# Two-layer diffusion trunk with 32 experts: adders and gathers in one work block per pair, a shorter layer step, full-width loads of the output weights

## The chip, the cores and the metric

One core of one Trainium2 chip runs the whole program. The time is in device microseconds (us) of one launch. The kernel before takes 1481.97 us, the median of 3 runs (1481.2 to 1482.17).

## What is computed

A trunk of two layers over 256 latent and 256 context tokens of width 1024, all in float32. Cut to what matters here:

```python
for i in range(2):                        # with_ctx_out = i < 1
    sh1, sc1, g1, sh2, sc2, g2 = split(silu(c) @ w_mod[i] + b_mod[i], 6)
    hl = modulate(rms_norm(x, norm1_g[i]), sh1, sc1)       # the same for xc with c_ctx
    lat_mix, ctx_mix = token_mixers(hl, hc, w_in[i], ..., sink[i], cos, sin, with_ctx_out)
    x = x + g1 * (lat_mix @ w_out[i])                      # 6 + 6 heads of 64 and 256 conv channels
    hl = modulate(rms_norm(x, norm2_g[i]), sh2, sc2)       # in layer 0 also the context
    y = hierarchical_moe(hl, w_group[i], b_group[i], w_expert[i], ..., w_gate[i], w_up[i], w_down[i])
    x = x + g2 * y                                         # top-1 of 4 groups, top-2 of its 8 experts
return rms_norm(x, final_g)
...
def run(xb, e):                            # for each expert
    return (silu(xb @ w_gate[e]) * (xb @ w_up[e])) @ w_down[e]
```

## The kernel before

The program is Python that emits instructions for the five engines; a scheduler puts them in order where no manual schedule is given. In layer 1 only the latent tokens go through the output projection and the experts.

**Storage.** `slot` hands out eight buffers of 1 MB in turn; nearly all weights pass through them, loaded on SP's queue in program order. Smaller loads use a pool of 512 KB tiles (`load_k4`). A weight's load waits for the last reader of its buffer.

**Number formats.** Exact float32 products run as float32 matmuls. Others split both sides into a high part that the faster format (`fp32r`) holds and the rest, and sum three products (high by high, high by low, low by high): `Splits` makes the parts of a weight on ACT (`wh`) and on DVE or POOL (`wl`).

**Startup.** Eleven small tables (the rotary table, then for each layer the q and k gains, two router biases and the sinks) are loaded on POOL's queue (L194 to L207), the sinks' negation `negsink` on POOL at L210. SP loads the first layer's modulation weights (`wm`), and in between `wkv` and `wU`, the weights of the first projections. `mod_load(...)` issues a modulation's loads and returns `compute`, which multiplies (`pm`, L281) and adds the bias. Between the two halves of layer 0's first modulation stand 20 dummy products (L584 to L586). The router's weights `wr` are loaded on POOL at each layer's start (L471, L472), though first read after the attention.

**Attention and output projection.** A unit takes two heads, j and 3 + j, of a group. `load_wo` (L922 to L933) therefore gathers the rows of w_out in nine loads, eight of them 64 partitions wide, at the end of SP's queue for this part.

**Experts.** 16 pairs a layer, in eight quads of two pairs; each pair streams 12 MB. `pair` multiplies gate (`pgu`, 32 machine products), then up, transposes the activations (`pat`), and multiplies down (`py`). Four bursts of other work stand in between: after gate, after up, after the transposes and half way through down. The list `at` (L1587 to L1596) fills them with the adders of the pair before (`row_adders`: per 128 output channels two products `pc` and two updates of the residual `xT` on DVE) and the gathers of the next quad's tokens (`pg`, L1285, L1286; ACT copies them to `xg`).

**Layer step.** The last pair of layer 0 goes through `finish` (L1533 to L1546): after each adder the residual is squared on ACT; POOL adds squares 1 to 3 to 0, and sums over channels are taken of five squares (`ss`, L418; four products each, which the trace counts as eight). Then comes layer 1's norm, `rb` (the norm spread over partitions), modulated tokens `hT`/`hL`, and the first projection `pkv` (L558). The modulation (1, 2), called `early`, fills TensorE's gaps.

Of the kernel before, what the change touches and what calls it, by code (L numbers as in the profile page):

```python
# [15 lines left out]
OP = mybir.AluOpType  # L16
# [20 lines left out]
def trunk(ctx: ExitStack, tc: tile.TileContext, t_in, rope, out, cfg):  # L37
# [156 lines left out]
    gp.dma_start(rope_t, rope)  # L194

    def bcast_load(t, src, n):
        gp.dma_start(t, bass.AP(tensor=src.tensor, offset=src.offset, ap=[[0, 128], [1, n]]))

# [3 lines left out]
    for l in range(DEPTH):  # L202
        bcast_load(gqk[:, l, 0, :], qg_d[l], 64)
        bcast_load(gqk[:, l, 1, :], kg_d[l], 64)
        bcast_load(rb[:, l, 0:4], bgrp_d[l], 4)
        bcast_load(rb[:, l, 4:36], bexp_d[l], 32)
        bcast_load(sinkb[:, l, :], sink_d[l], 6)  # L207
# [55 lines left out]
    def mod_load(l, m, c0, nc, load=load_k):  # L263
# [9 lines left out]
        def compute(two=False, eng=gp, between=None, p=None):  # L273
# [3 lines left out]
            for k in range(KC * nq // 4):  # L277
                for q in range(4):
                    kq = k + q // nq * 4
                    c = q % nq * n  # L280
                    pe.matmul(p[0][32 * q:32 * q + 32], scT[:, kq, :], ws[128 * kq // nr][:, kq % (nr // 128), c:c + n],  # L281
                              start=k == 0, stop=k == KC * nq // 4 - 1)
            s = K2("ms", (128, n), tag="m")
# [23 lines left out]

        return compute
# [99 lines left out]
    sums, ss1 = [], []  # L408
# [50 lines left out]
    def layer(l):  # L459
# [5 lines left out]
        r1 = rstd(ssq0 if l == 0 else ss1[0], 4, D, "n1")  # L465
        if l > 0:
            finish_mods(l, 1)
# [3 lines left out]
        gp.dma_start(wr[:, :, 0:4], wgrp_d[l].rearrange("(k p) g -> p k g", p=128))  # L471
        gp.dma_start(wr[:, :, 4:36], wexp_d[l].rearrange("(k p) g -> p k g", p=128))  # L472
        h_mul, h_scale, h_shift, hH, hL = modulate(l, r1)
# [21 lines left out]
        if l > 0:  # L495
            early = mod_load(*todo.pop(0), 0, 8)
        for j in range(4):
# [38 lines left out]
        if l > 0:  # L536
            h_mul(0)
            h_scale(0)
            ws = Splits(wKV, 512)
            trans.close()  # L540
            with tc.high_priority(offset=-cfg["fpri"]):
                early(True)
# [20 lines left out]
        if l == 0:  # L563
# [16 lines left out]

            modulation(0)
            mul_to(3)

            for _ in range(20):  # L584
# [1078 lines left out]
```

## Time and profile before

| | |
|---|---|
| median of 3 runs | 1481.97 us (1481.2 to 1482.17) |
| profiled execution: time, span | 1484.51 us, 1482.9 us |
| mean granted TensorE clock | 0.979 of full |
| busy: PE, DVE, ACT, POOL | 1410.0, 612.1, 394.6, 85.9 us |
| moved by DMA | 481.86 MB, mean 325 GB/s |

The span runs from the first to the last instruction of the profiled execution; some 1.6 us lie around it. Busy time is a mean over stages with different limits: the startup and layer 0's projections to about 150 us, attention and output projection to 297, layer 0's experts from 305 to 803, the layer step to 823, layer 1's mixers and router to 1020, and layer 1's experts to the end.

### The profile page before, as it was taken

Reading aid. Unit: us, or ns where it says so; the run is one execution under the profiler, and the core shown is the slowest. Engines: PE = TensorE matmul, PEld = TensorE weight load, DVE = VectorE, ACT = ScalarE, POOL = GpSimd, SP = SyncE. Lnnn points to the kernel's source line nnn. Section 1 sums busy time; section 2 is a strip of 40 time slices with the busy share of each in tenths; the row PEclk is TensorE's granted clock in tenths of the full one; section 3 lists DMA queues with packets and bytes.
Section 4 is the critical chain, followed back from the end, with each engine's and each line's share of the span. In section 5 each row is a group of like instructions: output and inputs, shape, how many; then the busy total and the mean of one; then the engine's idle time right before and its main releaser. Section 6 shows DMA issues by size and latency. Waiting matters only on the chain. (4 is left out here: it accounts for less than half of the span.)

```text
span 1482.9 us, 20526 instructions
## 1 busy us (share of the span) xinstructions
PE 1410.0 (95%) x8080; PEld 775.2 (52%) x8080; DVE 612.1 (41%) x1379; ACT 394.6 (27%) x954; POOL 85.9 (6%) x146
## 2 busy tenths in 40 slices
PE   6999899999999999998999998989999999999997
PEld 4777677754444544444435776774443343333432
DVE  3469884353223333333334568853222222222223
ACT  3454575430111111100102555652111111110102
POOL 3212000100000000000001020010000000000000
PEclk8999999999999999999999899999999999999999
DMA  9847502399799999999999583087999999999996
GB/s 312 315 156 260 138 2 103 153 359 371 319 402 411 415 409 407 417 408 397 390 401 383 203 292 89 4 361 290 371 419 422 420 421 422 421 420 421 420 418 257
DMA packets 92324, 481.86 MB, mean 325 GB/s; under 512 B 8884, under 2 KB 17296, under 8 KB 47040
## 3 DMA queue, kind: packets, MB, share of 16 engines
q1 hardware_dynamic: 90960, 478.19, 81.3%
q0 software_dynamic: 800, 1.20, 0.4%
q8 instruction: 66, 1.08, 0.3%
q10 hardware_dynamic: 464, 1.11, 0.2%
q14 instruction: 34, 0.28, 0.0%
HBM read 479.42 MB, written 1.05 MB: 324 GB/s over the span
## 5 line engine op out<-in xcount | busy, mean ns | idle before, releaser
L1340 PE MATMUL pgu<-we,xg 128*64 128x512 f32 x1904 | 450.8, 598 | 23.4 <-DMA we<-in_w_gate_dram 13.1
L1340 PEld LDWEIGHTS pgu<-we,xg 128*64 128x64 f32 x1904 | 143.5, 137 | 308.8 <-issue 251.6
L1394 PE MATMUL py<-we,actT 128*64 128x512 f32 x888 | 205.8, 597 | 0.7 <-ACT actT L1355 0.7
L1236 DVE SCALAR_TENSOR_TENSOR xT<-pc,mod,xT 128x256 f32<-128x256 f32 x256 | 104.8, 476 | 177.4 <-PE pc L1233 177.4
L1394 PEld LDWEIGHTS py<-we,actT 128*64 128x64 f32 x888 | 61.9, 136 | 114.8 <-issue 110.8
L1290 ACT COPY xg<-pg 128x256 f32<-128x256 f32 x112 | 36.3, 376 | 309.8 <-PE pg L1286 309.8
L1349 DVE SCALAR_TENSOR_TENSOR act<-pgu,ws,sil 128x512 f32<-128x512 f32 x32 | 24.0, 751 | 194.0 <-PE pgu L1340 185.1
L1244 DVE TENSOR_TENSOR xo<-xo,pc 128x512 f32<-128x512 f32 x62 | 39.8, 683 | 111.3 <-PE pc L1243 111.3
L1285 PE MATMUL pg<-OH,hH 128*128 128x256 f32 x336 | 84.2, 290 | 0.0
L1286 PE MATMUL pg<-OH,hL 128*128 128x256 f32 x336 | 81.7, 283 | 0.0
L634 DVE SCALAR_TENSOR_TENSOR ca<-gpad,cw,ca 128x512 f32<-128x512 f32 (+1 forms) x120 | 73.3, 611 | 0.9
L1285 PEld LDWEIGHTS pg<-OH,hH 128*128 128x128 f32 x336 | 64.2, 191 | 11.4 <-issue 10.5
L281 PE MATMUL pm<-wm,scT 128*32 128x256 f32 (+1 forms) x896 | 64.3, 370 | 2.2 <-DMA wm<-in_w_mod_dram 2.0
L1286 PEld LDWEIGHTS pg<-OH,hL 128*128 128x128 f32 x336 | 64.3, 191 | 0.0
L1344 ACT ACTIVATE sil<-pgu 128x512 f32<-128x512 f32 x32 | 19.2, 598 | 167.1 <-PE pgu L1340 167.1
L1259 DVE TENSOR_TENSOR Yg<-py,g2r 128x512 f32<-128x512 f32 x31 | 21.3, 688 | 100.8 <-PE py L1394 96.5
L1363 POOL CAST se<-ident 32x128 fp32r<-32x128 f32 x32 | 9.1, 286 | 900.8 <-PE pb L1364 871.0
L1261 ACT CAST YH<-py 128x512 fp32r<-128x512 f32 x32 | 18.7, 586 | 151.3 <-PE py L1394 134.4
L1261 ACT CAST YH<-Yg 128x512 fp32r<-128x512 f32 x31 | 19.1, 618 | 141.2 <-DVE Yg L1259 141.2
L1232 PE MATMUL pc<-oht,YH 128*128 128x512 f32 x128 | 55.2, 432 | 0.2 <-ACT YH L1261 0.2
L1233 PE MATMUL pc<-oht,YL 128*128 128x512 f32 x128 | 50.6, 395 | 0.2 <-DVE YL L1262 0.2
L1262 DVE TENSOR_TENSOR YL<-py,YH 128x512 fp32r<-128x512 f32 x32 | 22.1, 691 | 61.2 <-ACT YH L1261 61.2
(434 smaller groups left out, 2125.4 us busy)
## 6 DMA issues: line engine op xcount, KB each, us to landing
we<-in_w_up_dram SPq DMA_DIRECT2D x112, 1024.0 KB, 8.9
we<-in_w_down_dram SPq DMA_DIRECT2D x111, 1024.0 KB, 11.2
we<-in_w_gate_dram SPq DMA_DIRECT2D x110, 1024.0 KB, 11.8
wm<-in_w_mod_dram SPq DMA_DIRECT2D x44, 1024.0 KB, 11.0
wp<-in_w_gate_dram SPq DMA_DIRECT2D x8, 1024.0 KB, 11.2
wp<-in_w_up_dram SPq DMA_DIRECT2D x8, 1024.0 KB, 10.3
we<-in_w_gate_dram SPq DMA_DIRECT2D x16, 512.0 KB, 11.0
we<-in_w_up_dram SPq DMA_DIRECT2D x16, 512.0 KB, 10.2
```

Source lines behind the costliest of these rows:

```text
L281: pe.matmul(p[0][32 * q:32 * q + 32], scT[:, kq, :], ws[128 * kq // nr][:, kq % (nr // 128), c:c + n], start=k == 0, stop=k == KC * nq // ...
L634: ve.scalar_tensor_tensor(a, g, wt, a, op0=OP.mult, op1=OP.add)
L1232: pe.matmul(pc, YH[:, 128 * o:128 * o + 128], oht, start=True, stop=False)
L1233: pe.matmul(pc, YL[:, 128 * o:128 * o + 128], oht, start=False, stop=True)
L1236: ve.scalar_tensor_tensor(xT[:, o, sl], pc[:, sl], mod[l][:, 5, o, s:s + 1], xT[:, o, sl], op0=OP.mult, op1=OP.add)
L1244: ve.tensor_tensor(xo[t][:, sl], xo[t][:, sl], pc, op=OP.add)
L1261: sc.copy(YH[:rows, sl], py)
L1285: pe.matmul(dst, hH[t][:, 128 * k:128 * k + 128], rhs, start=t == 0, stop=False)
L1286: pe.matmul(dst, hL[t][:, 128 * k:128 * k + 128], rhs, start=False, stop=t == NT - 1)
L1290: sc.copy(xg[e][:, k - 1:k + 1, :], v[:, :, e])
L1340: pe.matmul(p[64 * e:64 * e + 64, m, :], xg[:, k, 64 * e:64 * e + 64], w_[e](k % 4), start=k == 0, stop=k == KC - 1)
L1394: pe.matmul(py[64 * e:64 * e + 64, h], actT[:, 128 * f + 64 * e:128 * f + 64 * e + 64], wd[e](f % 2)[:, 512 * h:512 * h + 512], start=f == ...
```

## The change

**Experts of layer 0**, the 13 pairs from the second to the fourteenth that gather for a next quad: gate and up run as one piece, down as one piece. All eight adders stand with the gathers between up and the down product: after up two adders, two gathers and two adders, after the transposes one adder, the other two gathers and three adders. The first pair, the last quad and layer 1 keep their order.

**Startup.** The eleven small loads go to SP, behind the last `wU`; `negsink` comes two operations later on POOL. Of the dummies 4 stand before the second half of the modulation and 12 after it. `wr` is loaded on SP ahead of `wo`.

**Heads** 2j and 2j + 1 make a unit, so w_out's rows are contiguous: five loads of 128 partitions in place of nine.

**Layer step.** The loads of modulation (1, 2) are named earlier (their place in SP's order is the same), its products stand between the sums; square 4 is added on POOL and squares 5 and 6 on DVE, so three squares are summed, not five; the weight splits of the first projection stand ahead of the norm; eight dummy products (`warm`) precede the first projection.

Core of the diff:

```diff
-    gp.dma_start(rope_t, rope)
...
-        gp.dma_start(t, bass.AP(tensor=src.tensor, offset=src.offset, ap=[[0, 128], [1, n]]))
...
-    gp.tensor_scalar(negsink, sinkb.rearrange("p l (h j) -> p l j h", h=2), -1.0, None, op0=OP.mult)
+    def bcast_load(t, src, n, eng=gp):
+        eng.dma_start(t, bass.AP(tensor=src.tensor, offset=src.offset, ap=[[0, 128], [1, n]]))
+
+    def small_inputs():
+        sp.dma_start(rope_t, rope)
+        for l in range(DEPTH):
+            bcast_load(gqk[:, l, 0, :], qg_d[l], 64, sp)
...
+            bcast_load(sinkb[:, l, :], sink_d[l], 6, sp)
+        gp.tensor_scalar(negsink, sinkb.rearrange("p l (j h) -> p l j h", h=2), -1.0, None, op0=OP.mult)
@@ mod_load
-        def compute(two=False, eng=gp, between=None, p=None):
+        def products(ks=range(KC * nq // 4), two=False, p=None):
...
+        def compute(two=False, eng=gp, between=None, p=None, made=None):
+            p = made or products(two=two, p=p)
@@ layer
-        gp.dma_start(wr[:, :, 0:4], wgrp_d[l].rearrange("(k p) g -> p k g", p=128))
-        gp.dma_start(wr[:, :, 4:36], wexp_d[l].rearrange("(k p) g -> p k g", p=128))
...
+        if l == 0:
+            small_inputs()
...
+        if l > 0:
+            ws = Splits(wKV, 512)
+        h_mul, h_scale, h_shift, hH, hL = modulate(l, rstd(ss1[0] if l else ssq0, 4, D, "n1"))
...
         if l > 0:
+            early[0].products(range(5, 8), p=early[1])
+            pw_ = P1("warm")
+            for _ in range(8):
+                pe.matmul(pw_[:, 0:256], identb, masks.rearrange("p a b -> p (a b)"), start=True, stop=True)
...
-                early(True)
+                early[0](made=early[1])
...
             modulation(0)
             mul_to(3)
-
-            for _ in range(20):
-                pe.matmul(pm[:, 1, 256:512], identb, masks.rearrange("p a b -> p (a b)"), start=True, stop=True)
+            dummies(4)
             modulation(1)
+            dummies(12)
@@ unit
-                    q = qT[g](3 * h + j, 128 * (i + b))
+                    q, kv = qT[g](2 * j + h, 128 * (i + b)), (2 * j + h) // 3
@@ load_wo
-            for n, part in enumerate((((0, 0, 2),), ((0, 128, 1), (1, 640, 1)), ((0, 704, 2),))):
-                for h in range(2):
-                    for i, r, m in part:
-                        r += 192 * h
-                        sp.dma_start(t[n][64 * h:64 * h + 64, i:i + m, :], src[r:r + 64 * m].rearrange("(j d) f -> d j f", d=64))
-            sp.dma_start(t[3], src[384:640].rearrange("(c p) f -> p c f", p=128))
+            for n in range(4):
+                c0, c1 = order[2 * n:2 * n + 2]
+                if c1 == c0 + 1:
+                    sp.dma_start(t[n], src[128 * c0:128 * c0 + 256].rearrange("(c p) f -> p c f", p=128))
+                else:
+                    for i, c in enumerate((c0, c1)):
+                        sp.dma_start(t[n][:, i], src[128 * c:128 * c + 128])
...
+        sp.dma_start(wr[:, :, 0:4], wgrp_d[l].rearrange("(k p) g -> p k g", p=128))
+        sp.dma_start(wr[:, :, 4:36], wexp_d[l].rearrange("(k p) g -> p k g", p=128))
         wo = load_wo()
@@ finish
-                    if o in (1, 2, 3):
+                    if o in (1, 2, 3, 4):
                         gp.tensor_tensor(sq_[0], sq_[0], q, op=OP.add)
+                    if o == 6:
+                        ve.tensor_tensor(q, sq_[5], q, op=OP.add)
                 if h == 1:
+
+                    f = mod_load(*todo.pop(0), 0, 8)
+                    made = f.products(range(2), two=True)
                     p = P1("ss1")
-                    for i, o in enumerate((0, 4, 5, 6, 7)):
-                        sum_tokens(p, sq_[o], NT, i == 0, i == 4)
+                    for i, o in enumerate((0, 7, 6)):
+                        sum_tokens(p, sq_[o], NT, i == 0, i == 2)
+                    f.products(range(2, 5), p=made)
@@ the bursts of a pair
-                    at = [adders[:3] + mine[:hot] if qd or e else [weights], mine[hot:6], adders[3:5], adders[5:]]
-                    at[3] += mine[6:]
-                    if not mine:
-                        at[1], at[2] = at[2], []
+                    if mine and not last:
+
+                        g = mine[hot:]
+                        head, g = (g[:1], g[1:]) if hot else ([], g)
+                        a_ = adders
+                        at = [mine[:hot], head + a_[:2] + g[:2] + a_[2:4],
+                              a_[4:5] + g[2:4] + a_[5:6] + g[4:6] + a_[6:7] + g[6:] + a_[7:], []]
+                    else:
...
```

How the order of instructions changes, at three places. The names are those of the tiles: `pgu` gate and up, `pc` adders, `pg` gathers, `pat` transposes, `pb` the pair's slots, `py` down.

PE, a second pair of a quad in layer 0, before:

```order
L1340 MATMUL pgu<-we,xg 64x512 x16
L1232 MATMUL pc<-oht,YH 128x512
L1233 MATMUL pc<-oht,YL 128x512
...
L1340 MATMUL pgu<-we,xg 64x512 x16
L1285 MATMUL pg<-OH,hH 128x256
L1286 MATMUL pg<-OH,hL 128x256
...
L1353 MATMUL pat<-ident,act 128x128 x4
L1232 MATMUL pc<-oht,YH 128x512
...
L1364 MATMUL pb<-posT,se 128x512
L1394 MATMUL py<-we,actT 64x512 x8
L1232 MATMUL pc<-oht,YH 128x512
...
L1394 MATMUL py<-we,actT 64x512 x8
```

and with the change:

```order
L1354 MATMUL pgu<-we,xg 64x512 x32
L1246 MATMUL pc<-oht,YH 128x512
L1247 MATMUL pc<-oht,YL 128x512
...
L1299 MATMUL pg<-OH,hH 128x256
L1300 MATMUL pg<-OH,hL 128x256
...
L1246 MATMUL pc<-oht,YH 128x512
...
L1367 MATMUL pat<-ident,act 128x128 x4
L1246 MATMUL pc<-oht,YH 128x512
...
L1299 MATMUL pg<-OH,hH 128x256
...
L1246 MATMUL pc<-oht,YH 128x512
...
L1378 MATMUL pb<-posT,se 128x512
L1408 MATMUL py<-we,actT 64x512 x16
```

Gate and up are one run of 32 products, and down one of 16 (the trace counts two machine products for each); the adders stand on both sides of the gathers in the one block between them.

PE, the layer step from the last down product to the first projection (`pm` modulation, `ss` sums of squares, `rb` the norm; the trace counts two machine products for each of `pm` and `ss`), before:

```order
L1370 MATMUL py<-we,actT 64x512 x4
L281 MATMUL pm<-wm,scT 32x256 x8
L1232 MATMUL pc<-oht,YH 128x512
...
L418 MATMUL ss_6622<-ones,sq 128x1 x4
L281 MATMUL pm<-wm,scT 32x256 x8
L418 MATMUL ss_6622<-ones,sq 128x1 x12
L281 MATMUL pm<-wm,scT 32x256 x3
L418 MATMUL ss_6622<-ones,sq 128x1 x4
L281 MATMUL pm<-wm,scT 32x256 x13
L339 MATMUL rb<-ident,n1r 128x128 x4
L291 MATMUL pm<-ident,ms 128x8 x2
L558 MATMUL pkv<-wh,hT 128x512 x4
```

and with the change, from the last adder on:

```order
L1246 MATMUL pc<-oht,YH 128x512
L1247 MATMUL pc<-oht,YL 128x512
L281 MATMUL pm<-wm,scT 32x256 x8
L423 MATMUL ss_6633<-ones,sq 128x1 x12
L281 MATMUL pm<-wm,scT 32x256 x12
L344 MATMUL rb<-ident,n1r 128x128 x4
L281 MATMUL pm<-wm,scT 32x256 x12
L542 LDWEIGHTS identb
L542 MATMUL warm<-masks,identb 128x256
...
L563 MATMUL pkv<-wh,hT 128x512 x2
L295 MATMUL pm<-ident,ms 128x8 x2
```

The sums are 12 in one piece, `rb` stands between two runs of 12 modulation products, and the dummies between the second run and `pkv`.

SP's queue ahead of the output projection, as the difference:

```order
 L85 DMA wm<-in_w_mod_dram 128x2x1024 x12
-L930 DMA wo<-in_w_out_dram 64x2x1024 x2
-L930 DMA wo<-in_w_out_dram 64x1024 x4
-L930 DMA wo<-in_w_out_dram 64x2x1024 x2
-L931 DMA wo<-in_w_out_dram 128x2x1024
-L1007 DMA xs<-in_w_down_dram 128x2048
+L978 DMA wr<-in_w_group_dram 128x8x4
+L979 DMA wr<-in_w_expert_dram 128x8x32
+L940 DMA wo<-in_w_out_dram 128x2x1024
+L943 DMA wo<-in_w_out_dram 128x1024 x2
+L940 DMA wo<-in_w_out_dram 128x2x1024 x2
```

The two loads of `wr` now come first, and each load of `wo` spans 128 partitions.

## Rows read from the trace of the kernel before

**Rows 1.** The page, traffic in 40 slices of 37 us, GB/s.
```profile
GB/s 312 315 156 260 138 2 103 153 359 371 319 402 411 415 409 407 417 408 397 390 401 383 203 292 89 4 361 290 371 419 422 420 421 422 421 420 421 420 418 257
```

**Rows 2.** Windows: length, busy us by engine (PE first), then PEclk, DMA share, GB/s.
```profile
498.47:529.47 31.00, 31.00 (x160) 14.80 (x157) 10.86 (x24) 3.56 (x8) 0.28 (x1) 1.00 1.00 406
529.47:559.58 30.11, 30.11 (x152) 13.91 (x150) 9.34 (x20) 3.56 (x8) 0.28 (x1) 1.00 1.01 414
1100.00:1350.00 250.00, 237.55 (x1075) 98.55 (x1073) 56.56 (x99) 30.75 (x69) 2.58 (x9) 1.00 1.01 421
```

**Rows 3.** Timeline of PE, pairs of layer 0: start, us, line, operation, tiles, count.
```profile
331.78 4.08 PE L1394 MATMUL py<-wp,actT 128*64 128x512 f32 x17 [0.25 <-ACT actT L1355]
338.70 0.60 PE L1340 MATMUL pgu<-we,xg 128*64 128x512 f32 x2
...
505.77 0.39 PE L1233 MATMUL pc<-oht,YL 128*128 128x512 f32 x1
506.00 0.39 PE L1232 MATMUL pc<-oht,YH 128*128 128x512 f32 x1
...
514.04 1.05 PE L1311 MATMUL pw<-whl,OH 128*128 128x4 f32 x8
520.81 3.65 PE L1394 MATMUL py<-we,actT 128*64 128x512 f32 x16
```

**Rows 4.** DMA view, 438 to 678 us (layer 0's experts), 40 slices of 6 us, GB/s.
```profile
GB/s 406 429 423 421 359 403 430 418 422 410 385 423 429 418 377 386 422 429 421 411 392 423 426 422 396 389 415 429 418 423 396 429 422 422 406 369 393 427 422 427
```

**Rows 5.** DMA view, 4 to 30 us, the POOL queue: packets, MB, share of 16 engines.
```profile
q0 software_dynamic: 576, 0.52, 17.1%
```

**Rows 6.** Startup: timeline of PE, ACT, SP and POOL, and one window (as rows 2).
```profile
21.95 4.01 PE L585 MATMUL pm<-masks,identb 128*128 128x256 bf16 x20 [0.26 <-DVE mod L298]
...
30.52 0.40 ACT L526 CAST wu<-wU 128x256 fp32r<-128x256 f32 x1 [0.76 <-DMA wU<-in_w_in_dram]
...
31.39 0.50 PE L558 MATMUL pkv<-wh,hT 128*128 128x512 f32 x1 [1.85 <-ACT hT L365]
...
39.73 1.84 SPq L91 DMA_DIRECT2D wU<-in_w_in_dram  x1
...
54.23 0.74 POOL L527 TENSOR_TENSOR wu<-wU,wu 128x256 fp32r<-128x256 f32 x1 [5.70 <-ACT wu L526]
...
32.50:36.00 3.50, 3.50 (x10) 2.71 (x9) 0.00 (x0) 0.00 (x0) 0.00 (x0) 0.51 1.05 387
```

**Rows 7.** Output weights: waits of 150 to 166, timeline of ACT, DMA from 144 to 172.
```profile
PE pT L843 <- ACT P L829: 5.2, 2, 4.1
...
158.66 1.14 ACT L380 CAST wh<-wo 128x512 fp32r<-128x512 f32 x2 [3.77 <-DMA wo<-in_w_out_dram]
...
GB/s 386 351 363 357 363 316 380 351 392 369 211 222 181 199 246 205 252 228 228 211 275 205 211 263 240 205 263 211 205 211 228 269 193 334 287 82 29 0 0 0
```

**Rows 8.** Layer step: timeline of DVE, PE and ACT, and the window of half clock.
```profile
806.03 3.22 DVE L1236 SCALAR_TENSOR_TENSOR xT<-pc,mod,xT 128x256 f32<-128x256 f32 x8 [0.59 <-PE pc L1233]
...
809.10 3.78 PE L418 MATMUL ss<-ones,sq 128*128 128x1 f32 x24
809.35 0.63 ACT L412 ACTIVATE sq<-xT 128x512 f32<-128x512 f32 x1 [0.15 <-DVE xT L1236]
...
813.81 1.87 PE L418 MATMUL ss<-ones,sq 128*128 128x1 f32 x8
...
815.61 3.62 PE L281 MATMUL pm<-wm,scT 128*32 128x256 f32 x26
...
819.16 1.12 PE L339 MATMUL rb<-ident,n1r 128*128 128x128 f32 x4
...
822.98 2.07 PE L558 MATMUL pkv<-wh,hT 128*128 128x512 f32 x4 [2.05 <-ACT wh L380]
...
810.80:827.80 17.00, 14.95 (x70) 10.78 (x70) 7.42 (x20) 6.06 (x15) 0.33 (x1) 0.50 1.04 369
```

**Rows 9.** DMA view of 806 to 816, 40 slices of 0.25 us, GB/s.
```profile
GB/s 451 328 434 340 397 397 328 381 340 365 352 352 344 352 348 344 352 344 348 352 373 254 332 213 139 250 139 213 305 285 285 334 365 346 422 352 350 358 371 371
```

More of the change, by code (lines that the diff above doesn't have):

```diff
@@ L276, in compute @@
                 p = p[:, 0:n], p[:, n:n + 16]
-            for k in range(KC * nq // 4):
+            for k in ks:
                 for q in range(4):
@@ L306, in compute @@
                 eng.tensor_tensor(A, A, g[:, :, None].to_broadcast([128, nc, 2]), op=OP.mult)
+        compute.products = products
         return compute
@@ L406, in trunk @@
     count = {}
-    sums, ss1 = [], []
+    sums, ss1, early = [], [], []
     def square(k, nt):
@@ L579, in splits, with dummies @@
                 su[k] = split_u(k, 0)
+            def dummies(n):
+                for _ in range(n):
+                    pe.matmul(pm[:, 1, 256:512], identb, masks.rearrange("p a b -> p (a b)"), start=True, stop=True)
             modulation(0)
             mul_to(3)
-            for _ in range(20):
-                pe.matmul(pm[:, 1, 256:512], identb, masks.rearrange("p a b -> p (a b)"), start=True, stop=True)
+            dummies(4)
             modulation(1)
+            dummies(12)
             splits(0)
@@ L805, in unit @@
                 for h in range(2):
-                    q = qT[g](3 * h + j, 128 * (i + b))
+                    q, kv = qT[g](2 * j + h, 128 * (i + b)), (2 * j + h) // 3
                     masked = g == 1 and i < 2
                     o, ks = (S[:, h, :], slice(0, 512)) if i < 2 else (S[:, h, 256 * b:256 * b + 256], slice(256, 512))
-                    pe.matmul(o, q, kH[g][:, h, ks], start=True, stop=False)
-                    pe.matmul(o, q, kL[g][:, h, ks], start=False, stop=not masked)
+                    pe.matmul(o, q, kH[g][:, kv, ks], start=True, stop=False)
+                    pe.matmul(o, q, kL[g][:, kv, ks], start=False, stop=not masked)
                     if masked:
@@ L860, in unit @@
             ve.tensor_tensor(rs, po[:, 0:nq], rs, op=OP.mult)
-            mh = qT[g](j, 128 * i, nq)
+            mh = qT[g](2 * j, 128 * i, nq)
             sc.copy(mh, rs)
-            ve.tensor_tensor(qT[g](3 + j, 128 * i, nq), rs, mh.bitcast(F32), op=OP.subtract)
+            ve.tensor_tensor(qT[g](2 * j + 1, 128 * i, nq), rs, mh.bitcast(F32), op=OP.subtract)
         conv(len(taps))
@@ L883, in mixed @@
             g, j = c // 5, c % 5
-            return qT[g](j, 0, N), qT[g](3 + j, 0, N)
+            return qT[g](2 * j, 0, N), qT[g](2 * j + 1, 0, N)
         def chunked(a):
@@ L1589, in layer @@
                     hot = 1 if len(mine) > 4 else 0
-                    at = [adders[:3] + mine[:hot] if qd or e else [weights], mine[hot:6], adders[3:5], adders[5:]]
-                    at[3] += mine[6:]
-                    if not mine:
-                        at[1], at[2] = at[2], []
+                    if mine and not last:
[5 more added lines that the diff above has]
+                    else:
+                        at = [adders[:3] + mine[:hot] if qd or e else [weights], mine[hot:6], adders[3:5], adders[5:]]
+                        at[3] += mine[6:]
+                        if not mine:
+                            at[1], at[2] = at[2], []
                     if qd == 0 and e == 0:
```

22 lines of the change are left out of this document (7 added, 15 removed).

## Prediction

> **What bounds the kernel now.** First the page's traffic in 40 slices: some 400 GB/s where experts are streamed, but 89 and 4 GB/s in slices 25 and 26 [rows 1]. So the last stage starts when TensorE's layer-1 work frees buffers, and what is saved ahead of it arrives at the end one for one. Then the windows: in layer 0's mixture of experts PE is busy in all of 31.00 and 30.11 us (a pair of each kind) while DMA moves 406 and 414 GB/s; in layer 1 DMA runs at 421 GB/s and PE has gaps [rows 2]. Layer 0's experts are PE's, layer 1's the memory's, with little between them. Outside, the timeline and the waits show three places where PE stands: before the first projection, at the output weights, at the layer step [rows 6 to 8]. A measurement tells about 0.2% (3 us) from no change.
>
> **The blocks of layer 0.** Before, six adder products split gate from up and six more split the down product. An adder product starts 0.23 after the one before it (505.77, 506.00) [rows 3]. A whole run of 32 products takes 6.92 (331.78 to 338.70, the first pair's down, unsplit). Gate and up with their adders took 514.04 - 498.47 (the first window's start) = 15.57, against 2 x 6.92 + 6 x 0.23 = 15.22; down with its adders 529.47 - 520.81 = 8.66, against 8.30. So each change between the two number formats and back costs about 0.35, and the change takes away two a pair: 0.70. The block between up and down exists already; adders that stand beside the gathers share its edges. DVE and ACT do the same work as before, in a place where PE doesn't wait for it.
>
> The limit is the memory: a pair reads twelve loads of 1.05 MB, 12.6 MB, at 421 GB/s 29.9 us, against (31.00 + 30.11)/2 = 30.55 now, so at most 0.65 can be had [rows 2]. Is 421 there? Slices of 6 us in this stage reach 430 between dips to 359 [rows 4]; a dip is DMA out of free buffers, so the 412 of the stage is PE's pace. I take 0.54 a pair, a little under the limit, for 13 pairs: **-7.0** (ends 0 and -8.4).
>
> The Trainium skill weighs on this. DMA: Bandwidth & Descriptors, section Specifications, gives a core about 358 GB/s from HBM; by that a pair would take an estimated 35 us, this stage would be DMA's already and the change worth 0. The trace disagrees: 421 GB/s for 250 us. The page's section Bandwidth has 425 for a core whose neighbour is idle; by it the limit is an estimated 29.6 us.
>
> **Startup.** ACT's first split of wU waits for its load until 30.52 and stands ahead of hT, which releases the first projection at 31.39; PE waits 1.9 for it [rows 6]. That chain hangs on loads. Between 4 and 30 us the POOL queue's packets took 17.1% of 16 engines, 4.4 us [rows 5]. Thirteen of its loads go behind the last wU or to attention, so what PE waits for lands up to 4.4 earlier. The twenty dummies took 4.01 (0.2 each); 16 remain, twelve of them between modulation and projection, into the gap of some 2 us that ACT's hT leaves; that can cost 0.5. They may keep the clock: between 32.5 and 36 it was granted 0.51 (the 1.2 GHz level), at which about 3.4 us of projection would have taken 1.7. Sum: -3.3 for loads (three quarters of 4.4), -1.2 for the clock, +0.5: **-4.0**, between -1 (only the clock) and -6.5 (everything). The late loads are first used on POOL: negsink, now behind four splits, waits for the last of them. They are issued behind the last wU, now at 39.73, and the split after negsink runs at 54.23; both move alike, so 14 us are left for them to land, and this costs nothing. If they land later, POOL's splits stop, and PE behind them as soon as POOL's lead is gone, us for us.
>
> **Output weights.** ACT's split waits 3.8 us for wo, and PE 4.1 of its 5.2 for the softmax behind that split [rows 7]. Traffic falls from some 360 to some 220 GB/s at 151.0 (144 + 10 slices of 0.7), where the 64-partition pieces begin, and the first slot is whole at 158.7, 7.7 later, since pieces of other slots move beside it. Full-width loads should run at 360 and one after the other: 2.9 for the first 1.05 MB. But the router's two loads, 2048 short runs, now go ahead on the same queue. At the layer step, where POOL issued them, ten slices fall from 350 to as low as 139 and lack some 0.25 MB, 0.8 us; against 400 GB/s the whole 10 us lack 1.7 [rows 9]. So the first slot would be whole at 154.7 to 155.6, 3 to 4 sooner, which is most of ACT's wait; the third split, now ahead of a softmax, takes 0.6 back, and PE's 4.1 shrink by some 2.5. As the short runs' price on this queue is open, I take **-2.0**. Upper end +3 (they cost 8 us there), lower end -4 (PE's wait gone).
>
> The Trainium skill speaks against this order: DMA: Bandwidth & Descriptors, section Specifications, wants at least 512 bytes a transfer for line rate. The runs here have 16 and 128. By the rule alone the term would lie at its upper end; the dip above agrees in kind, and no run here shows its size ahead of wo.
>
> **Layer step.** Before: eight residual updates on DVE from 806.03, sums of squares at 809.10 (24) and 813.81 (8), modulation products 815.61 to 819.16, broadcast rb, first projection 822.98 after ACT's split [rows 8]. After: 24 sums in place of 40; DVE adds one 512-column sum (0.7) ahead of the last two updates, so the last square ends at 811.4 instead of 810.0. Then 16 sums at 0.155 each (3.7/24, full clock) or 0.22 (1.8/8, half) end at 813.9 or 814.9, against 815.6. Behind them 24 modulation products (before: 26) stand ahead of rb, and 24 more with the eight dummies behind it; the weight split comes before the norm, so that hT alone releases the projection, some 3.2 after rb (822.98 - 819.16 less the split's 0.6). At full clock (half of 3.6/26 a product) rb starts at 815.5 and the projection at 818.7. If the half clock lasts as long as now, to 827.8, the products take 0.137 each (3.6/26) and PE itself is late: rb at 818.2, then 1.1 for rb, 3.3 for the products, 1.7 for the dummies (0.2 each, as in the startup): 824.3, which is 1.3 later than now. Full clock would also give back 2.3 on the projections up to 827.8. So the ends are +1.3 and -6.6. PE has no pause like the 2 us ahead of the projection now, which speaks for a shorter spell; if it ends near 817.6, rb comes near 818 and the projection near 821, and the projections run whole: -4. I take the middle of the ends: **-2.5**. The router's loads leave this stretch, where no wait depends on them: 0.
>
> **Edits at nothing.** Pairing heads as 2j, 2j+1 keeps the products' number and shape. Layer 1's wo has no wait row; should its splits come late, each us of it counts in full. The modulation loads for layer 1 keep their place on SP.
>
> **Sum.** -7.0 - 4.0 - 2.0 - 2.5 = -15.5. The profiled execution took 1484.5 (span 1482.9): 1469.0 by its own time, and 2.5 less by the median of the runs, 1482.0: **1466.5**.
>
> **Rivals.**
> 1. Memory becomes the bound in layer 0. For it: 412 GB/s is what the stage shows. If that is its own pace, the 7 us vanish and 8.5 remain: 1473.5. Against: the slices at 430. Chance 0.20.
> 2. The long block starves the queue, and the kernel is slower. The block grows from 6.8 us (514.04 to 520.81) by twelve adder products (2.8) to 9.6, in which no weight buffer comes free; there are eight of 1 MB, and DMA fills 3.9 in that time and 1.4 more before the first half of down is done. If it stands still p us in each pair, a pair takes 29.9 + p: no gain in the stage from 0.65, slower as a whole from 0.65 + 8.5/13 = 1.3. At p = 2: 13 x (29.9 + 2 - 30.55) = +17.5, less 8.5: +9.0, 1491. Against: 5.3 free buffers at the block's start are enough, and gate and up free eight in 13.8 us while 5.5 are filled, so they can be there. Chance 0.06.
> 3. The queue order doesn't do what it should: PE's start hangs on other things than bytes (-1), and short runs ahead of wo cost +3. Left: -7.0 - 2.5 - 1 + 3 = -7.5, 1474.5. For it: the landings are in order, and one late load holds all behind it; against: DMA's share is 1.05 at 32.5 to 36 [rows 6], so bytes are what it waits for. Chance 0.12.
>
> **Numbers.** Forecast 0.62, rivals 0.20, 0.06, 0.12. The range takes in rivals 1 and 3 (1473.5, 1474.5) and their own spread of some 3, and below the forecast three quarters of the 10 that the lower ends would add (-25.5 altogether): 1459 to 1478. Faster by over 0.2%: 0.87, which is 0.61 of the forecast and 0.26 of rivals 1 and 3, whose 7.5 to 8.5 us may shrink at other places; within: 0.06 from them; slower: 0.07, rival 2 and 0.01 of the forecast.
>
> **What would show it.** A pair in layer 0 near 30.0 us with DMA at 419 to 421 GB/s and PE without waits on DMA; PE's waits on we there would be rivals 1 or 2 (rival 2 if the rate has deep dips). First projection near 27.5, and no late POOL split. ACT's wait for wo under 2 us. From DVE's last eight updates to the first projection of layer 1 about 15 us instead of 17 (806.03 to 822.98), near 12.5 if the granted clock stays whole, over 17 if it stays half. Wrong altogether if the layer-0 pair stays over 30.5.

## The result, and the profile after

The changed kernel takes 1473.31 us (median of 4 runs, 1472.45 to 1474.36) against 1482.07 beside it (1481.2 to 1485.21): the ratio on record is 0.9926, with an interval of 0.9908 to 0.9945, which is 8 to 14 us less. By the two medians it is 8.8 us less, where 15.5 were forecast. The two profiled executions (1484.51 and 1472.71) lie 11.8 apart.

Where the two traces part, by the first or last machine product of a tile on PE:

| place | before | after | apart |
|---|---|---|---|
| first projection `pkv` | 31.39 | 26.32 | -5.1 |
| first query projection `pq` | 87.05 | 80.49 | -6.6 |
| first scores `S` | 148.88 | 142.26 | -6.6 |
| first output product `pwo` | 226.06 | 218.15 | -7.9 |
| first pair of layer 0, `pb` | 331.03 | 323.26 | -7.8 |
| last pair of layer 0, `pb` | 791.79 | 782.93 | -8.9 |
| first projection of layer 1 | 822.98 | 811.93 | -11.1 |
| last query projection of layer 1 | 904.69 | 891.03 | -13.7 |
| last output product of layer 1 | 989.10 | 977.05 | -12.1 |
| last product `pc` | 1473.82 | 1461.59 | -12.2 |

In these two executions the start won 6.6, the output weights 1.3, the experts of layer 0 some 1, the layer step 4.8; 1.6 went back in layer 1's attention. What other traces of the same parts show stands with the reasons below. The last stage passed the rest on unchanged.

**Experts of layer 0.** The windows of a pair of each kind, which answer to [rows 2], and of the stage:

```profile
427.58:458.85 31.27, 30.49 (x160) 15.01 (x158) 10.78 (x24) 3.65 (x8) 0.29 (x1) 1.00 1.00 404
458.85:489.21 30.36, 29.58 (x151) 14.11 (x149) 9.25 (x20) 3.66 (x8) 0.29 (x1) 1.00 1.00 413
438.00:678.00 240.00, 232.73 (x1192) 114.05 (x1190) 79.61 (x176) 28.64 (x63) 2.29 (x8) 1.00 0.99 409
```

A pair takes 31.27 and 30.36, where it took 31.00 and 30.11. PE, which was busy throughout, now lacks 0.78 us in each. ACT's `sil` is the silu of gate. The timeline of PE in the second of these pairs, which answers to [rows 3], shows where:

```profile
458.85 7.04 PE L1354 MATMUL pgu<-we,xg 128*64 128x512 f32 x32
466.67 7.09 PE L1354 MATMUL pgu<-we,xg 128*64 128x512 f32 x32 [0.78 <-ACT sil L1358]
473.68 0.50 PE L1246 MATMUL pc<-oht,YH 128*128 128x512 f32 x1
```

Gate takes 458.85 to 465.89 and its sum is then read by ACT; up starts 0.78 later. The waits of PE in the whole stage:

```profile
PE pgu L1354 <- ACT sil L1358: 10.3, 13, 1.1
PE pgu L1354 <- DVEq L1454: 1.5, 1, 1.5
```

13 waits, 10.3 us, on ACT's `sil`, and none on weights. So DMA pauses for PE as before; the rate, which answers to [rows 4], in the same 240 us:

```profile
GB/s 426 425 416 367 426 425 425 418 365 427 422 421 425 341 421 426 422 421 366 423 429 421 422 326 414 437 415 423 377 421 429 421 422 359 384 421 427 421 426 380
```

**Start.** Timeline and windows, which answer to [rows 6], and POOL's wait for the late sinks:

```profile
24.13 2.54 PE L589 MATMUL pm<-masks,identb 128*128 128x256 bf16 x12 [0.26 <-DVE mod L302]
...
24.86 0.40 ACT L528 CAST wu<-wU 128x256 fp32r<-128x256 f32 x1 [0.74 <-DMA wU<-in_w_in_dram]
...
26.32 0.78 PE L563 MATMUL pkv<-wh,hT 128*128 128x512 f32 x1
...
50.44 0.26 POOL L210 TENSOR_SCALAR negsink<-sinkb 128x12 f32<-128x12 f32 x1 [8.28 <-DMA sinkb<-in_sink_dram]
...
24.00:28.00 4.00, 3.87 (x16) 2.95 (x16) 1.81 (x4) 1.84 (x5) 0.73 (x1) 0.57 1.06 383
28.00:36.00 8.00, 7.99 (x87) 6.24 (x89) 3.10 (x6) 3.06 (x7) 1.48 (x2) 1.00 1.06 387
```

The twelve dummies now fill what was PE's wait, and the clock is whole from 28 on in this execution. `negsink` waits 8.3 us on POOL until 50.44, and PE doesn't wait for the splits behind it. The DMA view of 4 to 30 us, which answers to [rows 5]:

```profile
GB/s 309 397 378 354 400 412 404 373 344 371 394 381 384 394 384 381 394 384 381 397 381 381 400 381 356 369 369 372 380 359 358 364 391 389 378 391 391 378 391 388
...
q0 software_dynamic: 128, 0.07, 0.9%
```

**Output weights**, which answer to [rows 7]: a wait of PE, ACT's two places for splits, and the rate (40 slices of 0.7 us from 137.4, the same distance from the stage as before):

```profile
PE pT L853 <- ACT P L839: 3.4, 2, 2.3
...
149.73 1.14 ACT L385 CAST wh<-wo 128x512 fp32r<-128x512 f32 x2 [1.46 <-DMA wo<-in_w_out_dram]
...
151.46 0.64 ACT L385 CAST wh<-wo 128x512 fp32r<-128x512 f32 x1
...
GB/s 369 363 351 380 357 386 404 392 365 228 123 49 49 339 439 392 445 392 445 392 445 398 445 398 415 415 410 176 23 0 0 0 0 0 0 0 0 0 0 0
```

**Layer step**, which answers to [rows 8]:

```profile
797.18 2.44 DVE L1250 SCALAR_TENSOR_TENSOR xT<-pc,mod,xT 128x256 f32<-128x256 f32 x6 [0.59 <-PE pc L1247]
...
800.20 1.05 PE L423 MATMUL ss<-ones,sq 128*128 128x1 f32 x8 [0.67 <-POOL sq L1555]
...
802.64 3.57 PE L423 MATMUL ss<-ones,sq 128*128 128x1 f32 x16 [1.39 <-ACT sq L417]
...
806.14 2.79 PE L281 MATMUL pm<-wm,scT 128*32 128x256 f32 x24
...
808.86 0.67 PEld L344 LDWEIGHTS rb<-ident,n1r 128*128 128x128 f32 x4 [0.81 <-PE pm L281]
...
811.13 1.05 PE L542 MATMUL warm<-masks,identb 128*128 128x256 bf16 x8
...
811.93 0.70 PE L563 MATMUL pkv<-wh,hT 128*128 128x512 f32 x2
...
802.00:806.00 4.00, 3.36 (x16) 3.37 (x16) 1.29 (x2) 2.23 (x4) 0.00 (x0) 0.57 1.09 355
806.00:812.00 6.00, 6.00 (x62) 3.25 (x62) 2.35 (x9) 1.80 (x5) 0.00 (x0) 0.72 1.05 394
812.00:818.00 6.00, 6.00 (x31) 5.00 (x30) 4.71 (x12) 3.48 (x9) 1.79 (x2) 1.00 1.02 406
```

The 16 sums that are left start at 802.64, after a wait of 1.4 for the last square, during which the clock falls. A grant of 0.72 from 806 to 812 puts its return near 809.4, before the dummies, and the projections run whole. Before, half clock lasted until 827.8 [rows 8].

### The profile page after: what moved, and what is told of

It is laid out like the page before. It is cut to its first block, busy times and chain, and to the rows that moved or that the text cites. A ratio compares the mean times of both kernels' runs of the same rounds, so it can differ in the third digit from the quotient of the medians.

```text
span 1470.7 us, 20485 instructions
## 1 busy us (share of the span) xinstructions
PE 1390.8 (95%) x8068; PEld 771.3 (52%) x8068; DVE 613.4 (42%) x1380; ACT 395.7 (27%) x954; POOL 76.7 (5%) x132
## 3 DMA queue, kind: packets, MB, share of 16 engines
HBM read 479.42 MB, written 1.05 MB: 327 GB/s over the span
## 5 line engine op out<-in xcount | busy, mean ns | idle before, releaser
L1354 PEld LDWEIGHTS pgu<-we,xg 128*64 128x64 f32 x1904 | 142.3, 137 | 324.1 <-issue 246.8
L281 PE MATMUL pm<-wm,scT 128*32 128x256 f32 (+1 forms) x896 | 60.7, 359 | 3.0 <-DMA wm<-in_w_mod_dram 2.8
## 6 DMA issues: line engine op xcount, KB each, us to landing
we<-in_w_down_dram SPq DMA_DIRECT2D x111, 1024.0 KB, 12.4
we<-in_w_gate_dram SPq DMA_DIRECT2D x16, 512.0 KB, 12.1
```

Of the source, the lines that this page charges most:

```text
L1354: pe.matmul(p[64 * e:64 * e + 64, m, :], xg[:, k, 64 * e:64 * e + 64], w_[e](k % 4), start=k == 0, stop=k == KC - 1)
```

## The experiments

The theory after the traces: up's first product waits for ACT because gate and up are the two halves of one PSUM tile, and the wait is set for the tile. It always stood there; the six adder products behind gate (1.59 us) covered ACT's 0.6 us of reading. The change took the cover away. The rival: memory gives no more than 409 to 412 GB/s in this stage, and any wait on PE only takes the place of one for weights.

In diffs below, "..." leaves lines out. The scheduler orders the parts of the program that aren't ordered by hand anew for each kernel, so that small rearrangements in the two attentions come with most edits.

**Gate's sums in a tile of their own**

```diff
+            gate = P1("pgate") if own else None
             p = P2("pgu")
+            gu = [gate if own else p[:, 0], p[:, 1]]
...
-                            pe.matmul(p[64 * e:64 * e + 64, m, :], xg[:, k, 64 * e:64 * e + 64], w_[e](k % 4),
+                            pe.matmul(gu[m][64 * e:64 * e + 64, :], xg[:, k, 64 * e:64 * e + 64], w_[e](k % 4),
...
-                    sc.activation(sil, p[:, 0], AF.Silu)
+                    sc.activation(sil, gu[0], AF.Silu)
```

> The changed kernel, but gate's sums lie in a PSUM tile of their own in the 13 pairs with the new block, so up's first product no longer waits for ACT's read of gate. Theory (the wait): in the changed kernel up waits 0.78 us in each of 13 pairs, 10.3 us in all, which eats the 0.52 a pair that the block saves. Then a pair takes 30.04 us on the mean instead of 30.82, and the kernel about 10 us less than the changed one: 1463. Rival (memory): 409 GB/s is what memory gives in this stage, and PE's waits for ACT only stand where it would otherwise wait for weights. Then 1473, within 1.5, with waits on we in place of those on sil. In between, at 421 GB/s a pair can't be under 29.9, so not below 1461.

Measured: 1462.9 us, ratio 0.9849 (0.9823 to 0.9874), 10.4 less than the changed kernel. The first pair's `pb` to the last takes 450.0 us, where it took 459.7 in the changed kernel. PE's timeline in a pair, and the window of this stage:

```profile
456.22 7.04 PE L1355 MATMUL pgate<-we,xg 128*64 128x512 f32 x32
463.09 7.04 PE L1355 MATMUL pgu<-we,xg 128*64 128x512 f32 x32
...
430.00:670.00 240.00, 239.15 (x1214) 119.45 (x1212) 79.16 (x175) 29.24 (x64) 2.27 (x8) 1.00 1.01 418
```

Up follows gate without a wait, and DMA moves 418 GB/s. The theory holds; memory isn't the bound at 412. Up now starts 6.87 after gate (463.09 - 456.22), where it took 7.82 in the changed kernel (466.67 - 458.85): with what PE needs to start again the wait cost 0.95, more than the 0.78 it is listed with. PE's own work in a pair is then 30.82 - 0.95 = 29.87. Eight pairs in the middle take 30.17 on the mean, where 30.04 were expected, and twelve loads of 1.05 MB in 30.17 are 417 GB/s. Up's 32 products take 7.04 in four of the twelve pairs between 355 and 720 us and 7.15 to 7.81 in the others, while down's take 7.09 in all; in the pair of 520 to 530 PE waits 0.2 in the middle of up for its weights. So weights begin to bind here.

**Bursts as before**

```diff
-                    if mine and not last:
+                    if False:
```

> The changed kernel with the bursts of layer 0's pairs as before (six adder products after gate, the block after up, six in the middle of down); the other parts stay. Theory (the wait): the new block as it stands gains some 1 us in layer 0 against before (13 x 0.26 lost in the pairs, 2.3 won in the first ones, 2.2 behind the overflow branch), so this is 1 us slower than the changed kernel at most: 1473.5 to 1475. No wait on sil. Rival (memory): the same time, 1473, as both are at the memory's pace; then DMA moves as many GB/s as in the changed kernel.

Measured: 1476.03 us, ratio 0.9944 (0.9925 to 0.9963), 2.7 more than the changed kernel, where up to 2 were expected. The pairs are those of before, 31.00 and 30.11, and nothing waits for `sil`. The two intervals overlap: the new block as it stands is worth little either way. Of the 4.2 us that this trace loses against the changed kernel's, 1.2 lie in the stage itself (460.8 against 459.7 from the first `pb` to the last); 0.9 lie ahead of it, 1.3 in the layer step and 1.1 in layer 1's attention, where nothing was edited.

**Two adders between gate and up**

```diff
-                        at = [mine[:hot], head + a_[:2] + g[:2] + a_[2:4],
+                        at = [mine[:hot] + a_[:2], head + g[:2] + a_[2:4],
```

> The changed kernel with two of the eight adders (four products, 0.93 us) moved from the block to between gate and up, where they cover ACT's read of gate (0.78). Nothing else is added. Theory (the wait): the wait of 0.78 goes, one change of number format (0.35) comes back, so a pair is 0.43 shorter, 13 x 0.43 = 5.6: 1467.7. If the format change cost nothing it would be 1463, if it cost as much as the wait 1473. Rival (memory): 1473, as e1.

Measured: 1467.98 us, ratio 0.988 (0.9851 to 0.991), 5.3 less than the changed kernel. The timeline of PE:

```profile
458.80 7.04 PE L1354 MATMUL pgu<-we,xg 128*64 128x512 f32 x32
465.77 0.50 PE L1246 MATMUL pc<-oht,YH 128*128 128x512 f32 x1
...
466.57 0.40 PE L1247 MATMUL pc<-oht,YL 128*128 128x512 f32 x1
466.89 3.65 PE L1354 MATMUL pgu<-we,xg 128*64 128x512 f32 x16
```

Up starts 8.09 after gate, 0.93 of which is the adders' own work done earlier, with no wait: breaking the run costs 8.09 - 0.93 - 6.87 = 0.29, a little less than the 0.35 that the prediction put on the change of number format; no run tells the format's share from that of the break itself. A pair takes 30.61 and 29.72, 0.65 less than in the changed kernel, which is 0.95 - 0.29. The total is as forecast and 5 us above the run with the tile. But the pairs in the middle don't make those 5 us: (30.61 + 29.72)/2 is 30.17 too, at the same rate:

```profile
438.00:678.00 240.00, 236.48 (x1203) 113.96 (x1201) 78.88 (x172) 28.64 (x63) 2.27 (x8) 1.00 1.01 418
```

There two adders as cover do as well as the tile. The traces part by 1.6 ahead of the stage, by 3.7 in it (1.8 of that at the pair behind the overflow branch, where the program tests for tokens that don't fit an expert's slots) and by 2.0 in layer 1's attention, and 1.6 come back in the layer step; why isn't shown.

**Small loads back on POOL's queue**

```diff
-            bcast_load(gqk[:, l, 0, :], qg_d[l], 64, sp)
+            bcast_load(gqk[:, l, 0, :], qg_d[l], 64)
...
+    small_inputs()
...
-        if l == 0:
-            small_inputs()
```

> The changed kernel with the eleven small loads of the start back on POOL's queue ahead of everything (the router's weights stay on SP, the dummies as changed). Theory (bytes in the way): their packets took part of the 17 per cent of 16 engines that POOL's queue held from 4 to 30 us; the first projection comes some 3 to 5 us later than 26.3, and the kernel takes 1476 to 1478. Rival (the clock alone made the start faster, by the dummies' new place): 1473.5 at most, and the first projection within 1 us of 26.3.

Measured: 1477.73 us, ratio 0.9958 (0.9942 to 0.9974), 4.4 more than the changed kernel. Timeline of PE, and the DMA view of 4 to 30 us:

```profile
27.08 1.93 PE L282 MATMUL pm<-wm,scT 128*32 128x128 f32 x32 [0.53 <-DMA wm<-in_w_mod_dram]
...
30.04 1.47 PE L590 MATMUL pm<-masks,identb 128*128 128x256 bf16 x12 [0.26 <-DVE mod L303]
31.27 0.48 PE L564 MATMUL pkv<-wh,hT 128*128 128x512 f32 x1
...
GB/s 410 403 296 349 399 387 397 400 245 31 160 211 159 171 232 367 363 390 300 321 231 179 247 309 381 406 416 422 370 377 391 388 366 350 366 381 373 361 378 372
...
q0 software_dynamic: 496, 0.38, 16.9%
```

The first projection is back at 31.27, 4.95 later, though the dummies stand as changed; POOL's queue has 16.9% again and the rate falls below 200 in the same slices as before. Here the first twelve projection products run whole and take 2.9 us. At the first `pq` the trace is 4.4 behind the changed kernel's, as the median is: so 4.4 of the start is those loads.

**Twenty dummies between the halves of the modulation**

```diff
-            dummies(4)
+            dummies(20)
             modulation(1)
-            dummies(12)
```

> The changed kernel with all twenty dummies between the halves of the first modulation, as before, and none behind it. Theory (two separate gains at the start: bytes 4.4, clock 2.2): the first projection still starts near 26 to 27, but its first twelve products run at the half clock, 4.9 us instead of 3.5, and the twenty dummies stand in the second half's way for up to 1 us: 1474.5 to 1476. Rival (the dummies only fill a gap): 1473, no difference.

Measured: 1477.72 us, ratio 0.9968 (0.9956 to 0.998), 4.4 more; 1 to 2.7 were expected. Timeline of PE and the window of the first projections:

```profile
16.79 2.34 PE L589 MATMUL pm<-masks,identb 128*128 128x256 bf16 x20 [0.26 <-DVE mod L302]
...
25.61 0.80 PE L563 MATMUL pkv<-wh,hT 128*128 128x512 f32 x1 [1.85 <-ACT hT L370]
...
31.15 0.49 PE L535 MATMUL pu<-hT,wu 128*128 128x512 f32 x1
...
25.60:31.20 5.60, 5.59 (x13) 4.13 (x14) 1.21 (x3) 0.87 (x2) 0.36 (x1) 0.50 1.05 386
```

They start earlier, at 25.61, and the first twelve products take 5.5 us, at the half clock, instead of 3.5. By the first `pq` the trace is 1.4 behind the changed kernel's, by the first output product 2.8. The rest of the 4.4 isn't explained by this edit; in the trace 4.0 come at the pair behind the overflow branch, which takes 37.5 here and 33.4 in the changed kernel.

**No dummies in the layer step**

```diff
-            for _ in range(8):
-                pe.matmul(pw_[:, 0:256], identb, masks.rearrange("p a b -> p (a b)"), start=True, stop=True)
```

> The changed kernel without the eight dummies ahead of layer 1's first projection. Theory: the clock had come back at 809.3, before the dummies at 811.1, so they hold nothing; PE waits 0.8 us there instead, and the time stays within 1 us of 1473. Rival (the dummies keep the clock): the projections fall to half clock for at least 3.4 us and the kernel is 1.7 to 4 us slower, 1475 to 1477.

Measured: 1472.07 us, ratio 0.9924 (0.99 to 0.9948): 1.2 less than the changed kernel, with intervals that overlap: no difference that can be told. The dummies hold nothing.

**The layer step as before**

```diff
-                    if o in (1, 2, 3, 4):
+                    if o in (1, 2, 3):
...
-                    for i, o in enumerate((0, 7, 6)):
+                    for i, o in enumerate((0, 4, 5, 6, 7)):
...
+        if l > 0:
+            early = mod_load(*todo.pop(0), 0, 8)
...
-        if l > 0:
-            ws = Splits(wKV, 512)
```

> The changed kernel with the layer step as before (five squares summed, splits of the first projection's weight behind the norm, modulation products as the scheduler puts them, no dummies). Theory: the step is worth 5.9 us, so 1479; the half clock lasts some 17 us again, from before the sums to behind the first projections. Rival (the step's gain is given back in layer 1's attention, where the changed kernel loses 1.5): 1477 or less.

Measured: 1477.06 us, ratio 0.9965 (0.9949 to 0.9981), 3.8 more than the changed kernel; the traces part by 6.3. Timeline of PE and a window of 15 us:

```profile
811.35 1.12 PE L344 MATMUL rb<-ident,n1r 128*128 128x128 f32 x4
...
815.16 1.40 PE L561 MATMUL pkv<-wh,hT 128*128 128x512 f32 x4 [2.24 <-ACT wh L385]
...
805.00:820.00 15.00, 12.76 (x66) 8.93 (x66) 7.43 (x20) 6.15 (x15) 0.53 (x2) 0.66 1.05 393
```

The projection again waits 2.2 us for the weight split that stands behind the norm, and the clock is half for some 10 of the 15 us, not for the 17 that were expected. Of the 6.3 by which the traces part, 2.3 are there at the last pair of layer 0, ahead of the edit; 2.1 come between it and the last query projection of layer 1, and 1.9 in the attention behind it. The measured 3.8 lies at the rival's end. So the step is worth 2 us by this pair of traces and 4.8 by before and after; the size stays open between them.

**Gate's tile, and the router's loads behind the output weights**

```diff
+        wo = load_wo()
         sp.dma_start(wr[:, :, 0:4], wgrp_d[l].rearrange("(k p) g -> p k g", p=128))
         sp.dma_start(wr[:, :, 4:36], wexp_d[l].rearrange("(k p) g -> p k g", p=128))
-        wo = load_wo()
```

> The changed kernel with gate's sums in a PSUM tile of their own (as e1) and the router's two loads behind the output weights on SP in both layers. Theory: beside the 10.3 us of e1, ACT's wait of 1.5 us for wo goes, since the two loads held the queue for some 2 us of full rate; PE's wait of 2.3 us behind it shrinks by about as much: 1461. Rival (the third weight split or another wait takes its place): 1462.9, as e1; later if the router's weights come too late, which they have 90 us for.

Measured: 1464.82 us, ratio 0.9881 (0.9856 to 0.9905): 1.9 more than 1462.9, where 1.9 less was expected: no gain. ACT's wait for `wo` falls from 1.5 in the changed kernel to 1.1 only, and PE's longest for the softmax behind it stays 2.2, after 2.3. From the first scores to the first output product this trace takes 75.3 us, 0.9 less than the first run's, so the short runs cost the output weights 0.9 at most: in the changed kernel's slices above the rate falls to 49, and then runs at 392 to 445.

**The new block alone on the kernel before**

```diff
-                    at = [adders[:3] + mine[:hot] if qd or e else [weights], mine[hot:6], adders[3:5], adders[5:]]
...
+                    if mine and not last:
+                        g = mine[hot:]
...
```

> The kernel before with nothing changed but the order of the bursts in layer 0's 13 pairs (the new block). Theory (the wait on gate's tile): each pair loses 0.78 to the wait and gains 0.52, 0.26 slower in each of 13, so 1482 to 1485.5, with 13 waits on sil. Rival (the block gains by itself what was forecast, and the loss is made by other parts of the change): 1475.

Measured: 1483.17 us, ratio 1.0 (0.9986 to 1.0014). Waits of PE in the experts of layer 0, a window there and one in layer 1's output projection:

```profile
PE pgu L1340 <- ACT sil L1344: 10.0, 13, 0.8
...
438.00:678.00 240.00, 233.74 (x1196) 115.08 (x1194) 78.31 (x173) 29.22 (x64) 1.98 (x7) 1.00 0.99 410
972.00:982.00 10.00, 9.61 (x79) 8.89 (x76) 6.03 (x12) 7.99 (x15) 0.00 (x0) 1.00 1.00 422
```

The same thirteen waits. The block by itself moves nothing that can be measured, and the loss isn't made by other parts.

**The new block and gate's tile on the kernel before**

> The same (the kernel before with the new block alone), and gate's sums in a PSUM tile of their own. Theory: a pair takes 30.04 us instead of 30.55, 13 x 0.52 = 6.8 less: 1475.5, which is 10 less than the run without the tile; DMA near 418 GB/s in this stage. Rival (memory): within 1.5 of 1482, with waits on we.

The edit is the one above together with that of the first run. Measured: 1478.62 us, ratio 0.9973 (0.9962 to 0.9984), 4.6 less than without the tile, where 10 were expected. The stage did what it should: 453.5 us from the first pair's `pb` to the last, instead of 463.5 without the tile. The windows, to compare with the fence above:

```profile
438.00:678.00 240.00, 239.15 (x1214) 119.32 (x1212) 78.34 (x174) 29.16 (x64) 2.27 (x8) 1.00 1.01 417
963.00:975.00 12.00, 11.40 (x78) 10.65 (x79) 6.48 (x15) 8.19 (x15) 0.00 (x0) 0.73 1.01 427
```

In the same products of layer 1 the clock was 0.73 here and 1.00 there; from the last query projection to the last output product this trace takes 87.7 us and the other 84.1, so that 3.6 of the 10 are lost there. Why the clock fell there isn't settled; the scheduler's order in that part differs between the two.

**Gate's tile, no dummies in the layer step**

> The changed kernel with gate's sums in a PSUM tile of their own and without the eight dummies of the layer step. Theory: the two edits act at different places and add up: 1462.9 less what the run without the dummies gained (0 to 1.2), 1461.5 to 1463. Rival (the dummies hold the clock in some executions): 1463 to 1466.

Both edits are shown above. Measured: 1462.74 us, ratio 0.9871 (0.9855 to 0.9888). It equals the first run, as the theory said. These two are the fastest kernels of the study, 19 to 20 us under the kernel before and 10 under the changed one.

## Why the forecast was right in sign and too large

The measured time lies inside the stated 1459 to 1478, and that is in part luck. The largest term came to about nothing; the start and the layer step gave more than their terms, by 2.6 and 2.3 in the trace, and made up for some of it; and the upper part of the range had been drawn for rivals 1 and 3, neither of which happened.

The terms are compared below with the traces of before and after, which are one execution each. More traces have the same parts. The two runs on the kernel before (the new block alone, and with gate's tile) have its start, output weights and layer step; gate's tile, the bursts as before and the two adders have those of the change. Means, with the lowest and the highest, in us:

| stretch | as before, 3 traces | as changed, 4 traces | apart |
|---|---|---|---|
| to the first scores | 149.2 (148.9 to 149.6) | 143.0 (142.3 to 143.3) | -6.2 |
| from there to the first output product | 78.5 (77.2 to 79.8) | 76.3 (75.9 to 77.0) | -2.2 |
| last pair of layer 0 to last query projection of layer 1 | 112.2 (111.3 to 112.9) | 108.0 (106.5 to 109.4) | -4.2 |
| from there to the last output product | 85.4 (84.1 to 87.7) | 86.1 (84.6 to 87.1) | +0.7 |

**The block: -7.0 forecast, about nothing measured.** The step that failed reads: "DVE and ACT do the same work as before, in a place where PE doesn't wait for it." That is a statement about cover, and for the gate's read by ACT it was false. I had gone through what stands in the new block, and not through what stood in the place that the adders left. In the kernel before, ACT reads gate at 505.64 for 0.60 us, and up, behind the adders, starts at 507.02, when the read is over. One wait of its trace tells of the dependency even then: in layer 1's first pair, which has no adders between gate and up, up waits 0.2 us for `sil`. PE's timeline in layer 0, and PE's waits from 985 to 1042 us:

```profile
507.02 7.09 PE L1340 MATMUL pgu<-we,xg 128*64 128x512 f32 x32
...
PE pgu L1340 <- ACT sil L1344: 0.2, 1, 0.2
```

PE's side of the term held. Without the wait a pair saves 31.00 - (31.27 - 0.95) = 0.68 of PE's time, where the prediction had 0.70 ahead of the memory's limit. With the tile 30.55 - 30.17 = 0.38 a pair was left of it in the middle pairs, under the 0.54 that the prediction took after that limit. As the change stood, 13 x 0.68 = 8.8 against 13 x 0.95 = 12.4 makes +3.5 in the pairs. The run with the block alone, +0.5 with 2 us on either side, lies between that and the -1.1 of the trace, to which the pairs at the two ends of the new order and the branch contribute. A part of the stage's -1.1 in the trace is chance: the pair behind the overflow branch took 35.5 us before and 33.4 after, and anything from 33.2 to 37.5 in the profiled executions of this study, in whatever order.

**Rival 1 (memory), at 0.20, is out.** With PE's wait gone DMA moved 418 GB/s. The argument from the slices at 430 was right, and so was the answer to the Trainium skill's 358 GB/s for a core (DMA: Bandwidth & Descriptors, Specifications): both layers' experts stream above that, at 418 and 421. Rival 2 (a starved queue) left no wait on weights. My time of 1473.5 for rival 1 came close to the measured one for another reason, which the total alone doesn't tell.

**The start: -4.0 forecast, -6.6 in the trace.** Both mechanisms are there. The first projection comes 5.1 earlier, and the run that puts the loads back returns all but 0.1 of that there and 4.4 at the first `pq`, where I had taken three quarters of 4.4; the first twelve products then take 3.53 us instead of 4.90, so that the clock gives some 1.4 here, as the 1.2 said. That part is not steady: seven other traces with the same start take 3.26 to 4.49 for the twelve. The 0.5 for the dummies' place wasn't lost. The late `negsink` cost nothing, as said, though it used up the room: it held POOL from 42.2 to 50.44, and the next split ran at 50.68 where 54.23 less 6.6 would have been 47.6.

**The output weights: -2.0 forecast, -1.3 in the trace, -2.2 by the means.** ACT's wait fell from 3.8 to 1.5 and PE's longest from 4.1 to 2.3. The short runs weren't the price that I held back for; I had put 0.8 to 1.7 on them, and moving them away gave 0.9 in that stretch of a trace and nothing in the time. The Trainium skill (DMA: Bandwidth & Descriptors, Specifications) wants at least 512 bytes a transfer for line rate; the slices at 49 GB/s agree in kind, and the time hardly shows it.

**The layer step: -2.5 forecast, -4.8 in the trace, -4.2 by the means, 3.8 by the median of the run without it.** From the adders on DVE to the first projection it is 14.75 instead of 16.95, by the forecast's "about 15"; the clock was granted 0.72 from 806 to 812, half of 3.4 us, so it came back near 809.4, and the projections ran whole. That was the middle case, which I had priced at -4, and I took less.

**What was left out.** "Edits at nothing" had no term for layer 1's attention, which gives back 1.6 in the trace. PE waits there for `qT` at the output projection (1.2) and 0.5 longer for the convolution's norm. The waits for `qT` come with the scheduler's order and not with the pairing of heads: the kernel before with the new block alone has them, with the old pairing, and the changed kernel with gate's tile has none. Nor do they decide the stretch: with them the block alone passes it in 84.1, less than before's 84.4. The ranges in the table overlap, so it isn't shown that the change costs anything here. And the sum was made against one execution, 2.4 above the median of its kernel; the two traces lie 3 us further apart than the medians, and no stage of theirs is named for those 3.

## What to carry to other kernels

Before you move work away, list what it hid at the place that it leaves, not only what hides it where it goes: six adder products looked like an interruption and were the cover of a read that shares a tile with the next write. Where the cover must go, take the dependency away with it; a PSUM tile of its own for one of two accumulators took one of four small buffers, for which no wait appeared, and was worth 10 us, more than the change itself; two adders left in place did as well in the middle pairs. And when a term is right in size and the total isn't, look for the wait that appeared, by count: thirteen waits in thirteen pairs.

## What was not expected of the hardware

The pair behind the overflow branch took from 33.2 to 37.5 us in thirteen profiled executions with nearly the same work in it; the runs of one kernel spread by 2 to 9 us, and this is one place where it comes from: the two longest, 37.3 and 37.5, stand in executions 4.7 above the medians of their kernels. Small loads on POOL's queue hold back more than their bytes: 0.52 MB in 26 us [rows 5] went with a mean rate of 324 GB/s, and without most of them the same stretch moved 380, 1.4 MB more; with the eleven tables alone back (0.38 MB) it was 326. And 2048 runs of 16 and 128 bytes ahead of 4 MB of full-width loads pulled four slices down, to 49 GB/s at the lowest, and cost the wait behind them less than half a microsecond.
